# Routing of an expert-choice layer: a root moved to ScalarE and GpSimd, two conversions moved, fewer count products

## The chip, the cores and the metric

One core of a Trainium2 chip runs the whole layer in one launch. The metric is device time in microseconds (us). The runs of the kernel before have a median of 971.08 us.

The engines are TensorE (PE in the profile, its weight loads PEld), VectorE (DVE), ScalarE (ACT), GpSimd (POOL), and SyncE (SP), whose queue issues nearly all transfers. Each engine takes its instructions in the order in which the program gives them; a wait at the head of an engine's order holds everything behind it.

## The reference

An encoder layer on 512 tokens of 1024 features, in float32. Three attention branches are gated, summed and projected; the result is added to the residual and normalised. A mixture of 16 experts follows, in which each expert chooses its 64 best tokens, and a second normalisation. What this change touches lies between the two:

```python
x = layer_norm(DN_ALPHA * x + mix, ln1_g, ln1_b)          # mix = merged @ w_out
logits = jnp.einsum('btd,de->bte', x, w_router)
aff = jax.nn.softmax(logits, axis=-1)
gate, idx = lax.top_k(jnp.swapaxes(aff, 1, 2), 64)        # per expert
xs = x[bidx, idx]                                         # gathered tokens
h = jnp.einsum('becd,edf->becf', xs, w_gate_up)
hg, hu = jnp.split(h, 2, axis=-1)
ye = jnp.einsum('becf,efd->becd', jax.nn.silu(hg) * hu, w_down) * gate[..., None]
x = layer_norm(DN_ALPHA * x + zeros.at[bidx, idx].add(ye), ln2_g, ln2_b)
```

## The kernel before

Tokens stand in four chunks of 128 partitions. The order of work on every engine is written out by hand; no scheduler moves anything.

**Expert weights.** They come through a ring of twelve buffers, 2 MB or 1 MB each (class `Ring`, the transfers at L817). The queue of SyncE issues them in order, each when the buffer's last user is done. The first twelve are issued before the experts start; some of their buffers hold data of the routing first. The last of the twelve goes into the buffer of the normalised tokens `X1`, so it waits until the last chunk has been converted (L1073, the low parts). The next transfer goes into the ring's first buffer again and waits for the first two gate-and-up products (`gate_up`, L1285).

**Projection and statistics.** `w_rest` (L1104) does the second half of the output projection, chunk by chunk; the last chunk in two pieces of 256 columns. `wo_evac` (L1009) takes a piece out of PSUM, adds the residual and takes the statistics; `row_scale` (L1014) joins them and finds one over the root of the variance. It starts from an integer estimate and does three Newton steps: nine small operations on VectorE after the joining of the statistics. For the third chunk (`s2`) they alternate with the first rounds of the sort. `norm_cols` (L1060) makes the columns by which the tokens are normalised, on GpSimd; `x1_norm` (L1066) normalises a chunk on ScalarE.

**Router.** `r_transpose` (L989) transposes tokens on PE and copies them out by ScalarE; `r_logits` multiplies them with the router's weights; `affinity` (L1037) scales the logits on VectorE, takes the exponential on ScalarE and divides on VectorE. `r_back` (L1052) transposes the affinities of a chunk, so that experts lie on partitions, and ScalarE copies them out.

**Sort.** `rounds` (L1111) finds the 64 largest of each expert, eight at a time, on VectorE: first over chunks 0 and 1 (`seg`, beside the projection), then over chunks 2 and 3 with the first result's 64 (L1184 on). The 64th largest of each expert is `cut` (L1189). ScalarE makes a diagonal matrix `dg` of the cuts, and a product with ones spreads it over all partitions (`thp`, L1193).

**Counts.** VectorE compares affinities with the cut (L1197, L1198). PE counts chosen tokens ahead of each token by products with triangular and full matrices of ones: 16 products of 32 columns and 16 of 16 (L1202, L1205). VectorE turns the counts into positions and one-hot matrices (L1207 to L1223), and the gather is a product with these (`gather`, L1245 with the high parts of the tokens, L1247 with the low parts).

**High and low parts.** `x1_parts` (L1069) converts a normalised chunk to 16 bits on ScalarE (`XH`, L1070), and GpSimd subtracts and converts what is left (`XL`, two halves of 512, L1073).

**Keeping PE warm.** `keep_warm(n)` puts n products into PE's order whose result nobody reads. In the trace each shows as two matmuls.

Of the kernel before, what the change touches and what calls it, by code (L numbers as in the profile page):

```python
# [18 lines left out]
P = 128  # L19
# [3 lines left out]
NT = 4  # L23
NEXP = 16
# [40 lines left out]
def layer_kernel(ctx: ExitStack, tc: tile.TileContext, xt, xn, first0, wu, bgate, rpb, gains, wrt,  # L65
# [22 lines left out]
    def small(shape, name, dt=F32, bufs=2):  # L88
        return sp.tile(shape, dt, name=name, tag=name, bufs=bufs)
# [883 lines left out]
    def x1(m):  # L973
        return X1[:, m]
# [7 lines left out]
    nc.gpsimd.memset(a23, 0.0)  # L982
    top = cp.tile([48, 64], F32, name="top")

    XT, LG = {}, {}
    mvs, rs_v, rs_h, rs_y, rs_a, nmx, sme, rce = (
        small([P, NT, 2] if n == "mv" else [P, NT], "r_" + n, bufs=1) for n in ("mv", "v", "h", "y", "a", "nm", "sm", "rc"))
# [26 lines left out]
    def row_scale(ms, nq):  # L1014
        c = slice(ms[0], ms[-1] + 1)
        for m in ms:
            nc.vector.bn_aggr(mvs[:, m], st_all[:, m, :nq])
        yield
        v, hv, y, a = rs_v[:, c], rs_h[:, c], rs_y[:, c], rs_a[:, c]
        nc.vector.tensor_scalar(v, mvs[:, c, 1], LN_EPS, None, op0=ALU.add)  # L1020
        yield
        nc.vector.tensor_scalar(y.bitcast(I32), v.bitcast(I32), -0.5, RSQRT_SEED, op0=ALU.mult, op1=ALU.add)
        nc.vector.tensor_scalar(hv, v, -0.5, None, op0=ALU.mult)
        yield
        for i in range(3):
            if len(ms) == 1:
                nc.vector.tensor_scalar(a, y, hv, y, op0=ALU.mult, op1=ALU.mult)
                yield
                nc.vector.tensor_scalar(y, a, 1.5, y, op0=ALU.add, op1=ALU.mult)
            else:  # L1030
                nc.vector.tensor_tensor(a, y, y, op=ALU.mult)
                nc.vector.tensor_tensor(a, a, hv, op=ALU.mult)
                yield
                nc.vector.scalar_tensor_tensor(y, a, 1.5, y, op0=ALU.add, op1=ALU.mult)
            yield

    def affinity(ms):  # L1037
        ex = {m: LG[m][:, NEXP:2 * NEXP] for m in ms}
        for m in ms:
            nc.vector.scalar_tensor_tensor(lgA[:, m], LG.pop(m)[:, :NEXP], rs_y[:, m:m + 1], rb, op0=ALU.mult,  # L1040
                                           op1=ALU.add)
        c = slice(ms[0], ms[-1] + 1)
        nc.vector.tensor_reduce(nmx[:, c], lgA[:, c], axis=AX.X, op=ALU.max, negate=True)
        for m in ms:
            nc.scalar.activation(ex[m], lgA[:, m], AF.Exp, bias=nmx[:, m:m + 1], accum_out=sme[:, m:m + 1])
        yield
        nc.vector.reciprocal(rce[:, c], sme[:, c])
        for m in ms:
            nc.vector.scalar_tensor_tensor(aff[:, m], ex[m], rce[:, m:m + 1], ones_f[:, :NEXP], op0=ALU.mult, op1=ALU.mult)
        yield  # L1050

    def r_back(m):  # L1052
        ap = PB("Y", f"ap{m}")
        nc.tensor.transpose(ap[:NEXP, :P], aff[:, m], ident)
        p = 32 * (m % 2)
        nc.scalar.copy(a01[p:p + NEXP] if m < 2 else a23[p:p + NEXP, 64:], ap[:NEXP, :P])
# [3 lines left out]
    def norm_cols(ms):  # L1060
        c = slice(ms[0], ms[-1] + 1)
        nc.gpsimd.tensor_scalar(r13[:, c], rs_y[:, c], X_SCALE, None, op0=ALU.mult)
        for m in ms:
            nc.gpsimd.tensor_scalar(nb_t[:, m:m + 1], mvs[:, m, 0:1], r13[:, m:m + 1], -1.0, op0=ALU.mult, op1=ALU.mult)

    def x1_norm(m):  # L1066
        nc.scalar.activation(x1(m), x1(m), AF.Identity, bias=nb_t[:, m:m + 1], scale=r13[:, m:m + 1])

    def x1_parts(m):  # L1069
        nc.scalar.copy(XH[:, m], x1(m))  # L1070
        for h in range(2):
            c = slice(h * 512, h * 512 + 512)
            nc.gpsimd.tensor_tensor(XL[:, m, c], x1(m)[:, c], XH[:, m, c], op=ALU.subtract)  # L1073
# [66 lines left out]
    all_of(row_scale((0, 1), 2))  # L1140
    norm_cols((0, 1))
    w_rest(2, 0, 512, 1, {1: lambda: r_transpose(1, 4), 2: lambda: r_logits(1, 4),
                          3: lambda: all_of(affinity((0, 1)))})
    s2 = row_scale((2,), 2)
    seg = rounds(a01, 0, a23[:, 0:64], True)

    def sort_first():
        for _ in range(8):
            steps(s2, seg)

    w_rest(3, 0, 256, 1, {0: lambda: r_back(0), 1: then(lambda: r_back(1), sort_first), 2: lambda: r_transpose(2, 4),
                          3: lambda: r_logits(2, 4)})
    all_of(s2)
    x1_norm(0)
    norm_cols((2,))
    f2 = affinity((2,))

    def third():
        x1_norm(1)
        steps(f2)  # L1160
        all_of(seg)
        all_of(f2)

    w_rest(3, 256, 256, 2, {1: then(lambda: r_transpose(3, 4, 2), third), 2: lambda: r_logits(3, 4, 2)})
    keep_warm(3)
    r_transpose(3, 6, 2)
    r_back(2)
    r_logits(3, 6, 2)
    keep_warm(11)
    x1_parts(0)  # L1170
    all_of(row_scale((3,), 3))
    norm_cols((3,))
    all_of(affinity((3,)))
    r_back(3)
    x1_parts(1)
    for m in (2, 3):
        x1_norm(m)
        x1_parts(m)
    keep_warm(31)
    ring.upto(len(RING))  # L1180
    dump("aff", aff)

# [6 lines left out]
    nc.vector.tensor_reduce(cut, rev, axis=AX.X, op=ALU.min)  # L1189
    dg = cp.tile([NEXP, NEXP], F32, name="dg")  # L1190
    nc.scalar.activation(dg, ident[:NEXP, :NEXP], AF.Copy, scale=cut)
    thp = PB("S", "thp")
    nc.tensor.matmul(thp[:, :NEXP], ones_f[:NEXP], dg, start=True, stop=True)  # L1193
    keep_warm(1)
    msk = cp.tile([P, NT, 2, NEXP], F16, name="msk")
    thb = thp[:, None, :NEXP].to_broadcast([P, NT, NEXP])
    nc.vector.tensor_tensor(msk[:, :, 0], aff, thb, op=ALU.is_gt)  # L1197
    nc.vector.tensor_tensor(msk[:, :, 1], aff, thb, op=ALU.is_equal)  # L1198
    cnp = PB("S", "cnp", (P, NT, 2, NEXP))
    for m in range(NT):  # L1200
        for k in range(NT):
            nc.tensor.matmul(cnp[:, m].rearrange("p a e -> p (a e)"), tri_t[0 if k < m else 1 if k > m else 2],  # L1202
                             msk[:, k].rearrange("p a e -> p (a e)"), start=(k == 0), stop=False)
        for k in range(NT):
            nc.tensor.matmul(cnp[:, m, 1], ones_h, msk[:, k, 0], start=False, stop=(k == NT - 1))  # L1205
# [357 lines left out]
    for e in range(NEXP):  # L1563
# [71 lines left out]
    nc.vector.memset(ch[:, :, 7:9].bitcast(F32), 0.0)  # L1635
    warm_s = small([P, 1], "warm_s", bufs=1)
    nc.scalar.activation(warm_s, eps, AF.Sqrt)
    down(NEXP - 2, lambda: h_transpose(NEXP - 1, spare.rearrange("p (c n) -> p c n", c=4)))
    last_down(g2, {0: x0, 1: x1q}, spare)
# [141 lines left out]
```

## Time and profile before

| | us |
|---|---|
| median of 3 runs (971.02 to 971.66) | 971.08 |
| the profiled execution | 973.19 |
| its span, first to last instruction | 971.3 |
| PE busy (98% of the span) | 948.8 |
| VectorE busy (47%) | 454.8 |
| ScalarE busy (28%) | 276.0 |
| GpSimd busy (8%) | 79.3 |

Attention and projection take the first 506 us, the routing some 17 us, the experts and the last normalisation the rest. A row of the time-line has start, duration, engine, line, operation, result and operands, and in brackets the idle time before it with what ended it. A row of groups has the count, the busy time and the mean in ns, and the idle time before. Rows of windows are explained where they stand.

### The profile page before, as it was taken

Reading aid. Unit: us, or ns where it says so; the run is one execution under the profiler, and the core shown is the slowest. Engines: PE = TensorE matmul, PEld = TensorE weight load, DVE = VectorE, ACT = ScalarE, POOL = GpSimd, SP = SyncE. Lnnn points to the kernel's source line nnn. Section 1 sums busy time; section 2 is a strip of 40 time slices with the busy share of each in tenths; the row PEclk is TensorE's granted clock in tenths of the full one; section 3 lists DMA queues with packets and bytes.
Section 4 is the critical chain, followed back from the end, with each engine's and each line's share of the span. In section 5 each row is a group of like instructions: output and inputs, shape, how many; then the busy total and the mean of one; then the engine's idle time right before and its main releaser. Section 6 shows DMA issues by size and latency. Waiting matters only on the chain.

```text
span 971.3 us, 13273 instructions
## 1 busy us (share of the span) xinstructions
PE 948.8 (98%) x5444; PEld 619.5 (64%) x5444; DVE 454.8 (47%) x866; ACT 276.0 (28%) x544; POOL 79.3 (8%) x86
## 2 busy tenths in 40 slices
PE   9999999999999999999999999999999999998996
PEld 9899878889888888887886333433344333532344
DVE  6347668875376566237464122653322222231426
ACT  5334444544354454323223111100010001100123
POOL 0002303000032231000013000000000000000003
PEclk9999999999999999999999999999999999999998
DMA  9321111211333322575818999999999999999992
GB/s 360 111 68 65 65 66 44 66 46 64 85 112 112 100 82 83 218 285 201 366 61 340 406 431 430 431 430 430 431 431 429 430 431 430 430 429 430 429 396 89
DMA packets 38330, 251.21 MB, mean 259 GB/s; under 512 B 12911, under 2 KB 13295, under 8 KB 24830
## 3 DMA queue, kind: packets, MB, share of 16 engines
q1 hardware_dynamic: 37550, 249.74, 63.3%
q8 instruction: 43, 0.70, 0.3%
q10 hardware_dynamic: 720, 0.62, 0.2%
q14 instruction: 17, 0.14, 0.0%
HBM read 247.46 MB, written 2.10 MB: 257 GB/s over the span
## 4 chain that ended last, share of the span: by engine, by line
PE 80%; DMA 10%; DVE 6%; ACT 1%; issue 1%; POOL 1%; DVEq 0%; POOLq 0%; ACTq 0%; SPq 0%
DMA w<-in_wx 10%; PE g L1285 9%; PE u L1285 9%; PE y L1320 8%; PE gate L274 4%; PE gate L276 4%; PE gate L275 4%; PE pr L274 2%; PE gy L649 2%; PE ga L1245 2%; PE pr L275 2%; PE pr L276 2%; PE nqk L274 1%; PE nqk L275 1%; PE nqk L276 1%; PE gt L636 1%
## 5 line engine op out<-in xcount | busy, mean ns | idle before, releaser
L1285 PE MATMUL g<-w,xs 128*64 128x512 f32 x512 | 135.1, 606 | 3.6 <-DMA w<-in_wx 3.6
L1285 PE MATMUL u<-w,xs 128*64 128x512 f32 x512 | 131.6, 592 | 0.0
L1320 PE MATMUL y<-w,hT 128*64 128x512 f32 x480 | 106.8, 594 | 4.4 <-DMA w<-in_wx 3.7
L93 DVE TENSOR_TENSOR y<-y,y 64x512 fp32r<-64x512 f32 x30 | 20.7, 689 | 134.8 <-ACT y L92 134.8
L1285 PEld LDWEIGHTS u<-w,xs 128*64 128x64 f32 x512 | 36.8, 137 | 73.1 <-issue 72.3
L92 ACT CAST y<-y 64x512 fp32r<-64x512 f32 x30 | 17.4, 579 | 226.1 <-PE y L1320 214.8
L1320 PEld LDWEIGHTS y<-w,hT 128*64 128x64 f32 x480 | 33.7, 137 | 73.8 <-issue 63.2
L93 DVE TENSOR_TENSOR los<-raw_twin,whi 128x1024 fp32r<-128x1024 f32 x43 | 54.1, 1258 | 52.5 <-ACT whi L92 52.3
L276 PE MATMUL gate<-xh,los 128*128 128x512 f32 x192 | 74.8, 390 | 0.0
L1285 PEld LDWEIGHTS g<-w,xs 128*64 128x64 f32 x512 | 30.6, 136 | 55.0 <-issue 43.3
L274 PE MATMUL gate<-xh,whi 128*128 128x512 f32 x160 | 63.5, 397 | 0.0
L275 PE MATMUL gate<-xl,whi 128*128 128x512 f32 x160 | 62.3, 390 | 0.0
L1392 DVE TENSOR_TENSOR acc<-acc,cb 128x512 f32<-128x512 f32 x56 | 35.6, 684 | 37.7 <-PE cb L1390 37.7
L92 ACT CAST whi<-raw_twin 128x1024 fp32r<-128x1024 f32 x43 | 45.1, 1049 | 8.3 <-PE wo L1085 4.4
L93 DVE TENSOR_TENSOR los<-raw_twin,los 128x1024 fp32r<-128x1024 f32 x21 | 26.5, 1260 | 35.5 <-ACT los L92 35.4
L1461 POOL TENSOR_TENSOR acc<-acc,ln2g 128x512 f32<-128x512 f32 x6 | 7.6, 1276 | 432.7 <-DVE l2s L1489 430.7
L276 PEld LDWEIGHTS gate<-xh,los 128*128 128x128 f32 x192 | 36.0, 188 | 7.7
L625 ACT ACTIVATE att_twin<-gs,nm 128x512 f32<-128x512 f32 x32 | 21.7, 683 | 52.4 <-DVE nm L624 52.4
L1295 ACT ACTIVATE tg<-g 128x512 f32<-128x512 f32 x16 | 9.5, 597 | 90.2 <-PE g L1285 90.2
L274 PEld LDWEIGHTS gate<-xh,whi 128*128 128x128 f32 x160 | 30.0, 188 | 7.1 <-issue 1.2
L275 PEld LDWEIGHTS gate<-xl,whi 128*128 128x128 f32 x160 | 30.1, 188 | 5.9
L1308 DVE COPY hT<-ht 128x512 f32<-128x512 f32 x15 | 10.4, 691 | 44.4 <-PE ht L1303 44.4
(420 smaller groups left out, 1902.4 us busy)
## 6 DMA issues: line engine op xcount, KB each, us to landing
w<-in_wx SPq DMA_DIRECT2D x89, 2048.0 KB
raw_twin<-in_wu SPq DMA_DIRECT2D x65, 512.0 KB
w<-in_wx SPq DMA_DIRECT2D x14, 1024.0 KB
raw<-in_wu SPq DMA_DIRECT2D x8, 512.0 KB
xr<-in_xt SPq DMA_DIRECT2D x4, 512.0 KB
macc<-in_xn SPq DMA_DIRECT2D x2, 1024.0 KB
first<-in_first SPq DMA_DIRECT2D x4, 384.0 KB
bf<-in_rpb SPq DMA_DIRECT2D x64, 24.0 KB
```

Of the source, the lines that this page charges most:

```text
L92: nc.scalar.copy(hi, src)
L93: nc.vector.tensor_tensor(lo, src, hi.bitcast(F32), op=ALU.subtract)
L274: nc.tensor.matmul(acc, w_h, rh[:, k], start=(k == 0), stop=False)
L275: nc.tensor.matmul(acc, w_h, rl[:, k], start=False, stop=False)
L276: nc.tensor.matmul(acc, w_l, rh[:, k], start=False, stop=(k == nk - 1))
L625: nc.scalar.activation(self.p[:, h], self.s[h], AF.Exp, bias=nm[:, h:h + 1], accum_out=self.sm[:, h:h + 1])
L649: nc.tensor.matmul(self.y[h * 64:h * 64 + 64, :P], ST["vg"][:, kc, kvh * 64:kvh * 64 + 64], self.pt[:, h, kc], start=(kc == 0), stop=(kc = ...
L1245: nc.tensor.matmul(g, XH[:, m, c], oh[:, m, sl], start=(m == 0), stop=False)
L1285: nc.tensor.matmul(GU[e][b][hf * 64:hf * 64 + 64], xs, w[b][:, hf * 512:hf * 512 + 512], start=(k == 0), stop=(k == KD - 1))
L1308: nc.vector.tensor_copy(t, tp)
L1320: nc.tensor.matmul(y[o * 64:o * 64 + 64], hT[:, c, hf * 64:hf * 64 + 64], w[j][:, o * 512:(o + 1) * 512], start=(k == 0 and j == 0), stop= ...
L1392: nc.vector.tensor_tensor(a, a, cb, op=ALU.add)
```

## The change

- The third chunk's root, all nine operations, runs on GpSimd in place of VectorE, ahead of `norm_cols` in GpSimd's order. The affinities of that chunk wait for it.
- The last chunk's root is a square root on ScalarE, a reciprocal and one Newton step on VectorE. The square root needs another activation table than the exponential, so a table is loaded before it (with a warming call, right after the third chunk's normalisation) and the exponential's again after it.
- Normalisation of chunks 1 and 2 stands earlier in ScalarE's order.
- `r_back(2)` moves behind the last logits and stands next to `r_back(3)`; on ScalarE its copy comes behind the last exponential.
- The conversions `XH` of chunks 0 and 1 run on GpSimd.
- No diagonal: the cut itself, repeated along the columns without a copy, is the stationary operand, and the identity the moving one.
- The counts are formed by 14 products of 32 to 96 columns: one stationary matrix serves several chunks, the mask being repeated.
- Fewer warming products: 2, 5 and 28 in place of 3, 11 and 31.

```diff
+    eps = small([P, 1], "eps", bufs=1)
+    nc.gpsimd.memset(eps, LN_EPS)
+    warm_s = small([P, 1], "warm_s", bufs=1)
...
         v, hv, y, a = rs_v[:, c], rs_h[:, c], rs_y[:, c], rs_a[:, c]
-        nc.vector.tensor_scalar(v, mvs[:, c, 1], LN_EPS, None, op0=ALU.add)
-        nc.vector.tensor_scalar(y.bitcast(I32), v.bitcast(I32), -0.5, RSQRT_SEED, op0=ALU.mult, op1=ALU.add)
-        nc.vector.tensor_scalar(hv, v, -0.5, None, op0=ALU.mult)
+        eng = nc.gpsimd if len(ms) == 1 else nc.vector
+        eng.tensor_scalar(v, mvs[:, c, 1], LN_EPS, None, op0=ALU.add)
+        eng.tensor_scalar(y.bitcast(I32), v.bitcast(I32), -0.5, RSQRT_SEED, op0=ALU.mult, op1=ALU.add)
+        eng.tensor_scalar(hv, v, -0.5, None, op0=ALU.mult)
         for i in range(3):
             if len(ms) == 1:
-                nc.vector.tensor_scalar(a, y, hv, y, op0=ALU.mult, op1=ALU.mult)
-                nc.vector.tensor_scalar(y, a, 1.5, y, op0=ALU.add, op1=ALU.mult)
+                eng.tensor_scalar(a, y, hv, y, op0=ALU.mult, op1=ALU.mult)
+                eng.tensor_scalar(y, a, 1.5, y, op0=ALU.add, op1=ALU.mult)
...
+    def last_scale(m, nq):
+        c = slice(m, m + 1)
+        y, a, hv = rs_y[:, c], rs_a[:, c], rs_h[:, c]
+        nc.vector.bn_aggr(mvs[:, m], st_all[:, m, :nq])
+        nc.scalar.activation(rs_v[:, c], mvs[:, m, 1:2], AF.Sqrt, bias=eps)
+        nc.vector.tensor_scalar(hv, mvs[:, m, 1:2], LN_EPS, -0.5, op0=ALU.add, op1=ALU.mult)
+        nc.vector.reciprocal(y, rs_v[:, c])
+        nc.vector.tensor_scalar(a, y, hv, y, op0=ALU.mult, op1=ALU.mult)
+        nc.vector.tensor_scalar(y, a, 1.5, y, op0=ALU.add, op1=ALU.mult)
...
-    def x1_parts(m):
-        nc.scalar.copy(XH[:, m], x1(m))
+    def x1_parts(m, copy=nc.scalar.copy):
+        copy(XH[:, m], x1(m))
...
-    s2 = row_scale((2,), 2)
+    row_scale((2,), 2)
+    norm_cols((2,))
...
         for _ in range(8):
-            steps(s2, seg)
+            steps(seg)
...
-    all_of(s2)
     x1_norm(0)
-    norm_cols((2,))
+    x1_norm(1)
     f2 = affinity((2,))
 
     def third():
-        x1_norm(1)
         steps(f2)
...
-    keep_warm(3)
+    x1_norm(2)
+    nc.scalar.activation(warm_s, eps, AF.Sqrt)
+    keep_warm(2)
     r_transpose(3, 6, 2)
-    r_back(2)
+    last_scale(3, 3)
     r_logits(3, 6, 2)
-    keep_warm(11)
-    x1_parts(0)
-    all_of(row_scale((3,), 3))
+    keep_warm(5)
+    x1_parts(0, nc.gpsimd.tensor_copy)
     norm_cols((3,))
     all_of(affinity((3,)))
+    r_back(2)
     r_back(3)
-    x1_parts(1)
-    for m in (2, 3):
-        x1_norm(m)
-        x1_parts(m)
-    keep_warm(31)
+    x1_parts(1, nc.gpsimd.tensor_copy)
+    x1_parts(2)
+    x1_norm(3)
+    x1_parts(3)
+    keep_warm(28)
...
-    cut = small([NEXP, 1], "cut", bufs=1)
+    cut = cp.tile([NEXP, NEXP], F32, name="cut")[:, :1]
     nc.vector.tensor_reduce(cut, rev, axis=AX.X, op=ALU.min)
-    dg = cp.tile([NEXP, NEXP], F32, name="dg")
-    nc.scalar.activation(dg, ident[:NEXP, :NEXP], AF.Copy, scale=cut)
     thp = PB("S", "thp")
-    nc.tensor.matmul(thp[:, :NEXP], ones_f[:NEXP], dg, start=True, stop=True)
+    nc.tensor.matmul(thp[:, :NEXP], cut.to_broadcast([NEXP, P]), ident[:NEXP, :NEXP], start=True, stop=True)
...
-    for m in range(NT):
-        for k in range(NT):
-            nc.tensor.matmul(cnp[:, m].rearrange("p a e -> p (a e)"), tri_t[0 if k < m else 1 if k > m else 2],
-                             msk[:, k].rearrange("p a e -> p (a e)"), start=(k == 0), stop=False)
-        for k in range(NT):
-            nc.tensor.matmul(cnp[:, m, 1], ones_h, msk[:, k, 0], start=False, stop=(k == NT - 1))
+    for k in range(NT):
+        nc.tensor.matmul(cnp[:, k], tri_t[2], msk[:, k], start=(k == 0), stop=False)
+    for k in range(NT):
+        for lo, hi, t in ((0, k, 1), (k + 1, NT, 0)):
+            if lo < hi:
+                nc.tensor.matmul(cnp[:, lo:hi], tri_t[t], msk[:, k:k + 1].to_broadcast([P, hi - lo, 2, NEXP]),
+                                 start=False, stop=False)
+    for k in range(NT):
+        nc.tensor.matmul(cnp[:, :, 1], ones_h, msk[:, k, 0:1].to_broadcast([P, NT, NEXP]), start=False, stop=(k == NT - 1))
...
-    eps = small([P, 1], "eps", bufs=1)
-    nc.vector.memset(eps, LN_EPS)
...
-    warm_s = small([P, 1], "warm_s", bufs=1)
```

More of the change, by code (lines that the diff above doesn't have):

```diff
@@ L1017, in row_scale @@
             nc.vector.bn_aggr(mvs[:, m], st_all[:, m, :nq])
-        yield
         v, hv, y, a = rs_v[:, c], rs_h[:, c], rs_y[:, c], rs_a[:, c]
-        nc.vector.tensor_scalar(v, mvs[:, c, 1], LN_EPS, None, op0=ALU.add)
-        yield
-        nc.vector.tensor_scalar(y.bitcast(I32), v.bitcast(I32), -0.5, RSQRT_SEED, op0=ALU.mult, op1=ALU.add)
-        nc.vector.tensor_scalar(hv, v, -0.5, None, op0=ALU.mult)
-        yield
+        eng = nc.gpsimd if len(ms) == 1 else nc.vector
+        eng.tensor_scalar(v, mvs[:, c, 1], LN_EPS, None, op0=ALU.add)
+        eng.tensor_scalar(y.bitcast(I32), v.bitcast(I32), -0.5, RSQRT_SEED, op0=ALU.mult, op1=ALU.add)
+        eng.tensor_scalar(hv, v, -0.5, None, op0=ALU.mult)
         for i in range(3):
             if len(ms) == 1:
-                nc.vector.tensor_scalar(a, y, hv, y, op0=ALU.mult, op1=ALU.mult)
-                yield
-                nc.vector.tensor_scalar(y, a, 1.5, y, op0=ALU.add, op1=ALU.mult)
-            else:
[L1031 to L1035, printed above, removed]
+                eng.tensor_scalar(a, y, hv, y, op0=ALU.mult, op1=ALU.mult)
+                eng.tensor_scalar(y, a, 1.5, y, op0=ALU.add, op1=ALU.mult)
+            else:
+                eng.tensor_tensor(a, y, y, op=ALU.mult)
+                eng.tensor_tensor(a, a, hv, op=ALU.mult)
+                eng.scalar_tensor_tensor(y, a, 1.5, y, op0=ALU.add, op1=ALU.mult)
+    def last_scale(m, nq):
[7 more added lines that the diff above has]
+        nc.vector.tensor_scalar(y, a, 1.5, y, op0=ALU.add, op1=ALU.mult)
     def affinity(ms):
@@ L1139, in layer_kernel @@
     w_rest(1, 0, 512, 1, {1: lambda: r_transpose(0, 4), 3: lambda: r_logits(0, 4)})
-    all_of(row_scale((0, 1), 2))
+    row_scale((0, 1), 2)
     norm_cols((0, 1))
```

## The prediction

> **What bounds the kernel now.** I read the windows first, then the time-line around the routing, then the waits of the queue that loads the expert weights. Windows: start and end, PE, PEld, DVE, ACT and POOL busy, PEclk, DMA share, GB/s.
>
> ```profile
> span 971.3 us, 13273 instructions
> ...
> 518.90:520.00 1.10, 1.08 (x34) 0.90 (x34) 0.27 (x2) 0.00 (x0) 0.50 (x1) 1.00 0.10 30
> ...
> 526.00:528.00 2.00, 2.00 (x16) 0.79 (x14) 0.00 (x0) 0.37 (x1) 0.00 (x0) 1.00 0.04 16
> ...
> 530.00:541.00 11.00, 11.00 (x69) 4.02 (x70) 2.12 (x9) 2.01 (x5) 0.00 (x0) 1.00 0.99 380
> 528.00:943.00 415.00, 406.38 (x2044) 155.47 (x2042) 125.77 (x223) 47.20 (x86) 0.00 (x0) 1.00 1.01 428
> ```
>
> From 528 to 943 the DMA engines are full at 428 GB/s. PE also counts as busy nearly throughout, but it cannot finish before the last weights land, so the end is the moment at which the stream restarts, plus the rest of the weights, plus a tail that this change barely touches. Before 528 there are two holes: 518.9 to 520.0 and 526 to 528.
>
> ```profile
> 521.79 0.38 PE L1247 MATMUL ga<-oh,xhl 128*128 128x128 f16 x4
> 522.01 0.39 PE L1245 MATMUL ga<-oh,xhl 128*128 128x128 f16 x4
> ...
> 522.68 1.08 PE L1285 MATMUL g<-w,xs 128*64 128x512 f32 x4
> ...
> 526.01 1.03 PE L1285 MATMUL u<-w,xs 128*64 128x512 f32 x4
> ```
> ```profile
> SPq L817 <- POOL xhl L1073: 2.4, 1, 2.4
> ```
>
> The second hole ends when the first 2 MB ring block has been used: its last matmul ends at 526.01 + 1.03 = 527.04, and data flow again at 528. The first hole ends when GpSimd has written the last of the low parts (the queue waits 2.4 us for it; that load is the last one into the ring). So an earlier first gate matmul (522.68) moves the restart and the end one for one, as long as the load held by GpSimd has landed before the restart. That load fills the 6 us from 520 to 526. If it started right at 518.9 it would land before 525, so up to about 3 us of gain the DMA engines set no limit. What sets 522.68 is a chain through the routing. I cost each edit on this chain.
>
> **Third chunk's root off VectorE.** Times are start and duration.
>
> ```profile
> 498.84 0.21 DVE L1017 BATCH_NORM_AGGREGATE r_mv<-rt 128x2 f32<-128x12 f32 x1
> ...
> 502.88 0.20 DVE L1029 TENSOR_SCALAR r_y<-r_a,r_y 128x1 f32<-128x1 f32 x1
> 503.11 0.23 DVE L1040 SCALAR_TENSOR_TENSOR rt<-lg,r_y,rt 128x16 f32<-128x16 f32 x1
> ...
> 506.09 0.41 DVE L1011 SCALAR_TENSOR_TENSOR macc<-macc,woc 128x256 f32<-128x256 f32 x1
> ```
> ```profile
> 505.53 0.28 PE L1085 MATMUL woc<-wlast,ml 128*128 128x256 f32 x1
> ```
> ```profile
> 503.17 0.22 POOL L1062 TENSOR_SCALAR lnr<-r_y 128x1 f32<-128x1 f32 x1 [8.10 <-DVE r_y L1029]
> 503.48 0.27 POOL L1064 TENSOR_SCALAR lnnb<-r_mv,lnr 128x1 f32<-128x1 f32 x1
> ```
>
> The last projection matmul ends at 505.53 + 0.28 = 505.81, but VectorE takes its result only at 506.09, being behind with sort rounds and the root. Eight of the nine root operations stand where VectorE catches up by 502.08 anyway; the ninth, at 502.88, costs its pitch of 0.23 (502.88 to 503.11). Without it the evacuation starts at 505.86: **gain 0.23**, at most 0.28.
>
> The new wait: the logits' scaling (503.11, then 502.88) waits for nine one-column operations on GpSimd, and behind it in VectorE's order stand four sort rounds and the evacuation of the last chunk. Dependent one-column operations on GpSimd are 0.31 apart (503.17 to 503.48). Two pointer operands may make some 0.42, so nine take 2.8 to 3.3: from 499.14 to 501.9 or 502.4. The cover is 0.5 to 1.0; beyond it each microsecond on GpSimd is one at the end.
>
> **Last chunk's root.** Nine VectorE operations become a square root on ScalarE, a reciprocal and two operations of a Newton step (the fifth VectorE operation hides beside the square root).
>
> ```profile
> 507.00 0.24 DVE L1017 BATCH_NORM_AGGREGATE r_mv<-rt 128x2 f32<-128x18 f32 x1
> 507.09 0.37 ACT L996 COPY x1T<-x1t 128x256 f32<-128x256 f32 x1 [2.20 <-PE x1t L994]
> ...
> 507.36 0.25 ACT L1056 COPY a<-ap 16x128 f32<-16x128 f32 x1
> ...
> 508.83 0.27 DVE L1027 TENSOR_SCALAR r_a<-r_y,r_h 128x1 f32<-128x1 f32 x1
> 509.13 0.21 DVE L1029 TENSOR_SCALAR r_y<-r_a,r_y 128x1 f32<-128x1 f32 x1
> 509.45 0.23 DVE L1040 SCALAR_TENSOR_TENSOR rt<-lg,r_y,rt 128x16 f32<-128x16 f32 x1
> ...
> 509.93 0.28 ACT L1045 ACTIVATE lg<-rt,r_nm 128x16 f32<-128x16 f32 x1 [1.37 <-DVE r_nm L1043]
> ```
> ```profile
> 931.72 1.28 ACT L1637 ACT_TABLE_LOAD   x1
> 933.34 0.20 ACT L1637 ACTIVATE warm_s<-eps 128x1 f32<-128x1 f32 x1 [0.34 <-DVE ch L1635]
> ...
> 959.66 0.30 ACT L1513 ACTIVATE l2v<-l2mv,eps 128x4 f32<-128x4 f32 x1 [1.88 <-DVE l2mv L1511]
> ```
> ```profile
> 960.02 0.17 DVE L1517 RECIPROCAL l2y<-l2v 128x4 f32<-128x4 f32 x1
> 960.23 0.16 DVE L1518 TENSOR_TENSOR l2a<-l2y 128x4 f32<-128x4 f32 x1
> ```
>
> Everything is 0.23 earlier, so the statistics are ready at 507.01 and ScalarE starts the transposed copy at 506.86. It takes its next operation 0.27 after (507.09 to 507.36): square root at 507.13. Its nearest row is the one-column square root of 0.20 at 933.34; the hand-over to VectorE is 0.06 (959.66 + 0.30 to 960.02). So the reciprocal starts at 507.39, the Newton step at + 0.21 (960.02 to 960.23), its second half at + 0.30 (508.83 to 509.13), the scaling of the logits at + 0.32 (509.13 to 509.45): 508.22, against 509.45. The exponential follows 0.48 later: 508.70. The table load for the exponential starts when the square root ends, 507.33, and takes 1.28: 508.61, hidden by 0.09. If the 0.34 between the load and the next operation at 933.34 belonged to the load, the exponential would start at 508.95. **Gain at the exponential, with the 0.23: 509.93 - 508.70 = 1.23**; ends 0.98 and 1.32 (the load alone).
>
> The other table load, before the square root, must fit between the third chunk's normalisation and the transposed copy.
>
> ```profile
> 503.36 1.25 ACT L1067 ACTIVATE macc<-macc,lnnb,lnr 128x1024 f32<-128x1024 f32 x1
> ```
>
> In the new order the third chunk's exponential takes the slot at 503.4 in which the second normalisation stood (with its sum about 0.4, an estimate from the 0.28 at 509.93), and the third normalisation (1.25) runs from 503.8 to 505.05; load to 506.33; warming square root, 0.20, to 506.53; the copy is due at 506.86. It fits with 0.33 to spare.
>
> [...]
>
> The transposition of the third chunk's affinities moves behind the last logits, and its copy behind the last exponential: some 509.1 to 509.4, before the last chunk's transposition (about 509.7). Free. The sort has the same rounds.
>
> **No diagonal.**
>
> ```profile
> 517.78 0.21 DVE L1189 TENSOR_REDUCE cut<-rev 16x1 f32<-16x64 f32 x1
> ```
> ```profile
> 518.03 0.31 ACT L1191 ACTIVATE dg<-ident,cut 16x16 f32<-16x16 f32 x1 [0.53 <-DVE cut L1189]
> ```
> ```profile
> 518.39 0.29 PEld L1193 LDWEIGHTS thp<-dg,rt 16*128 16x128 f32 x2 [0.45 <-ACT dg L1191]
> ```
> ```profile
> 506.56 0.20 PEld L994 LDWEIGHTS x1t<-ident,macc 128*128 128x128 f32 x2 [0.27 <-DVE macc L1011]
> ```
>
> The cut ends at 517.99; ScalarE and two hand-overs lie before 518.39. Straight from VectorE to PE takes 0.06 (506.09 + 0.41 to 506.56), up to 0.12: 518.05 to 518.11. **Gain 0.31**, 0.28 to 0.34.
>
> **14 count products for 32.**
>
> ```profile
> 519.22 0.18 PE L1202 MATMUL cnp<-msk,tri_d 128*128 128x32 f16 x1
> ...
> 519.92 0.24 PE L1205 MATMUL cnp<-msk,ones_h 128*128 128x16 f16 x4
> ```
>
> Thirty-two products start from 519.22 to about 519.99, 0.025 apart whatever their 32 or 16 columns. A wide one goes by columns: four of 128 columns take 0.22 (521.79 to 522.01), 0.43 ns each. The new first thirteen are four of 32 columns (0.025 each), six of 96, 32, 64, 64, 32 and 96 (0.041, 0.025, 0.028, twice over, 0.19 in all) and three of 64 (0.08): 0.37 in place of 0.77. **Gain 0.40**, 0.30 to 0.45.
>
> **Two conversions to GpSimd.** They leave ScalarE, where they weren't late; the question is whether GpSimd becomes late.
>
> ```profile
> L1073 POOL TENSOR_TENSOR xhl<-macc,xhl 128x512 f16<-128x512 f32 x8 | 9.0, 1155 | 6.0 <-ACT xhl L1070 6.0
> ...
> L268 POOL TENSOR_SCALAR gT<-lnT 128x8 f32<-128x8 f32 x1 | 1.1, 1120 | 0.2 <-DMA lnT<-in_lnt 0.2
> ...
> L245 POOL TENSOR_SCALAR consts<-consts 128x64 f32<-128x64 f32 x1 | 0.4, 400 | 24.0 <-DMA consts<-in_gains 24.0
> masks.py:199 POOL TENSOR_SCALAR_AFFINE_SELECT ident<-ident 128x128 f32<-128x128 f32 x1 | 0.3, 292 | 0.1
> ```
>
> No row has this conversion (128x1024). From below: 128 elements in 0.29 against 0.22 for one column, about 0.6 ns each, 0.8 us. From above: 64 elements took 0.40, so 0.18 more than one column, 2.9 ns each, 3.1 us. I take 1.3: the two-input rows (1155 ns for 512, so 2.3 us for 1024 with two reads) are nearest in size, and this has one read for two. [...]
>
> GpSimd now starts when the last projection matmul frees the buffer, 505.9, 2.7 earlier than before. Its queue: conversion, two subtractions, two small operations, conversion, six subtractions: 505.9 + 2 x 1.3 + 8 x 1.155 - 0.1 + 0.6 = 518.2. The gather needs the last low part at 521.79 - 1.9 = 519.9, so the cover is 1.7 us; it is gone at 2.15 per conversion, and at 3.1 GpSimd ends at 521.8. With 1.3 the held load follows at 518.9 without a hole.
>
> **Sum.** 1.23 + 0.31 + 0.40 = 1.94 us earlier at the first gate matmul, 520.74, and at the restart (526.1). Nothing downstream takes it back: PE and DMA both start from there. The profiled execution took 973.19 against its span of 971.3; the runs' median is 971.08. I subtract from the median: 971.08 - 1.94 = 969.1; a profiled span of 969.4. The ends of the terms sum to 1.56 and 2.11, with the runs' spread: 968.7 to 969.8. For the chances, 0.2% is 1.94 us, about what a measurement of this kernel can tell from no change; the forecast sits on that bound.
>
> **Rivals.**
> *Table changes cost more than their row.* If each took twice its 1.28, the first would end at 505.05 + 2.57 + 0.20 = 507.8, the copy would be 0.96 late, the square root end at 508.3 and the exponential start at 510.9: 0.9 later than before, less the 0.71 of the other edits: 971.3. For it: two changes stand on a tight path. Against: 931.72. [...] Chance 0.06.
>
> *Conversions late.* Between 2.15 and 3.1 us each, GpSimd delivers after 519.9 and each 0.1 costs 0.2 at the gather: 969.3 to 971.1. For it: the 2.9 ns slope. Against: the affine select. Chance 0.06.
>
> *More than the sum.* From 530 to 541 the stream ran at 380 against 428 GB/s, 11 x 48 / 428 = 1.2 us lost. If that is the late held load's doing, landing it before 525 regains it: 967.9. Against: those loads are issued one by one, as PE frees blocks. Chance 0.14.
>
> *Slower: the third chunk's root stalls VectorE.* If GpSimd's operations take what its first small one took (1.12), nine last 10.1 us, to 509.2, and the scaling due at 502.88 holds sort and evacuation: 6.3 later, less 1.94: 975.5. It decides from 0.42 each on (nine in the 3.74 from 499.14 to 502.88), cancels the gain at 0.63 and passes 0.2% slower at 0.85. For: one operation works on integers, of which no GpSimd row exists. Against: 0.22 and 0.27. Chance 0.10.
>
> **Numbers.** Forecast 0.64, of which 0.34 beyond 0.2% and 0.30 short of it. Faster 0.34 + 0.14 = 0.48; within 0.2%: 0.30 + 0.06 + 0.06 = 0.42; slower 0.10. Range 968.0 to 971.3: it leaves out the slower rival and the edge of the better one.
>
> **What would show it.** Right: evacuation at 505.86, exponential at 508.7, no gap after its table load, weight load of the cut within 0.12 of its reduction, counts read 0.6 after the first product, GpSimd done by 518.9, the hole at 518.9 closed and data flowing again at 526.1. Wrong: VectorE idle at 502.9 waiting for GpSimd; the transposed copy later than 506.9; the gather waiting for the low parts; or the restart early and the end not.

## The result: 967.9 us, a quarter of a per cent faster

| kernel | median, us | runs | lowest and highest |
|---|---|---|---|
| before | 969.77 | 9 | 968.86 to 971.66 |
| after | 967.90 | 9 | 967.16 to 969.25 |

The ratio is 0.9975, with a 95% interval of 0.9966 to 0.9983: 2.4 us (1.6 to 3.3) of 969.77. The medians differ by 1.87. The forecast gain was 1.94; the forecast time was 969.1 with a range from 968.0, so the time fell 0.1 below the range. The three runs of the kernel before known at the prediction had a median of 971.08; with nine it is 969.77.

The profiled execution of the kernel after took 967.9 us, with a span of 966.1. Its windows, with the columns as in the prediction:

```profile
518.90:520.00 1.10, 1.10 (x8) 0.29 (x4) 0.47 (x3) 0.16 (x1) 0.00 (x0) 1.00 1.00 402
...
522.40:523.90 1.50, 1.50 (x14) 0.65 (x12) 0.00 (x0) 0.33 (x1) 0.00 (x0) 1.00 0.19 76
530.00:541.00 11.00, 11.00 (x70) 4.03 (x68) 3.55 (x11) 1.56 (x4) 0.00 (x0) 1.00 0.96 375
```

The first hole is closed: the DMA share from 518.9 to 520 is 1.00, where it was 0.10, and the lowest microsecond from 512 to 521 is 0.72, against 0.11 in the kernel before. The second stands earlier and ends at about 523.9, 5.3 after the first gate matmul at 518.62; before it ended at 528, 5.3 after 522.68. From 530 to 541 the stream is as slow as it was (375 against 380 GB/s). Counted from the first gate matmul the same eleven microseconds are those from 526 to 537, and there it ran at 383.

The time-line of the same kernel around the routing, TensorE first (last matmul of the projection, spread of the cut, first count products, first gate matmul), then VectorE:

```profile
503.36 0.28 PE L1093 MATMUL woc<-wlast,ml 128*128 128x256 f32 x1
...
514.71 0.39 PE L1200 MATMUL thp<-ident,cut 16*128 16x16 f32 x2 [0.59 <-DVE cut L1198]
...
515.54 0.25 PE L1208 MATMUL cnp<-msk,tri_d 128*128 128x32 f16 x4
...
518.62 1.08 PE L1295 MATMUL g<-w,xs 128*64 128x512 f32 x4
```
```profile
500.70 0.22 DVE L1048 SCALAR_TENSOR_TENSOR rt<-lg,r_y,rt 128x16 f32<-128x16 f32 x1
...
503.67 0.42 DVE L1014 SCALAR_TENSOR_TENSOR macc<-macc,woc 128x256 f32<-128x256 f32 x1
...
506.37 0.17 DVE L1051 TENSOR_REDUCE r_nm<-rt 128x1 f32<-128x16 f32 x1
...
514.44 0.21 DVE L1198 TENSOR_REDUCE cut<-rev 16x1 f32<-16x64 f32 x1
...
515.13 0.22 DVE L1204 TENSOR_TENSOR msk<-rt,thp 128x64 f16<-128x64 f32 x1 [0.48 <-PE thp L1200]
...
516.14 0.29 DVE L1217 TENSOR_TENSOR rt<-cnp,msk 128x128 f32<-128x128 f32 x1 [0.66 <-PE cnp L1215]
```

ScalarE, from the third chunk's normalisation to the last exponential, and GpSimd, from the third chunk's root to the last low part:

```profile
501.48 1.23 ACT L1075 ACTIVATE macc<-macc,lnnb,lnr 128x1024 f32<-128x1024 f32 x1
502.73 1.28 ACT L1173 ACT_TABLE_LOAD   x1
504.02 0.20 ACT L1173 ACTIVATE warm_s<-eps 128x1 f32<-128x1 f32 x1
504.68 0.37 ACT L999 COPY x1T<-x1t 128x256 f32<-128x256 f32 x1 [0.45 <-PE x1t L997]
504.95 0.30 ACT L1039 ACTIVATE r_v<-r_mv,eps 128x1 f32<-128x1 f32 x1
505.26 1.28 ACT L1053 ACT_TABLE_LOAD   x1
506.58 0.28 ACT L1053 ACTIVATE lg<-rt,r_nm 128x16 f32<-128x16 f32 x1
```
```profile
496.96 0.23 POOL L1023 TENSOR_SCALAR r_v<-r_mv 128x1 f32<-128x1 f32 x1 [4.07 <-DVE r_mv L1020]
...
499.94 0.27 POOL L1029 TENSOR_SCALAR r_y<-r_a,r_y 128x1 f32<-128x1 f32 x1
...
503.65 1.04 POOL L1078 CAST xhl<-macc 128x1024 f16<-128x1024 f32 x1 [2.79 <-ACT macc L1075]
...
508.78 6.74 POOL L1081 TENSOR_TENSOR xhl<-macc,xhl 128x512 f16<-128x512 f32 x6
```

The mask and the reading of the counts in the kernel before:

```profile
518.81 0.22 DVE L1197 TENSOR_TENSOR msk<-rt,thp 128x64 f16<-128x64 f32 x1 [0.82 <-PE thp L1193]
...
520.20 0.29 DVE L1207 TENSOR_TENSOR rt<-cnp,msk 128x128 f32<-128x128 f32 x1 [1.03 <-PE cnp L1205]
```

The projection ended at 503.64 here and at 505.81 in the profile of before, so the two are compared from that moment. Each row of this table is a difference of two starts or ends above and in the prediction:

| us | before | after | gain | forecast |
|---|---|---|---|---|
| end of projection to its evacuation | 0.28 | 0.03 | 0.25 | 0.23 |
| end of projection to last exponential | 4.12 | 2.94 | 1.18 | 1.23 |
| reduction of the cut to the mask | 1.03 | 0.69 | 0.34 | 0.31 |
| first count product to the counts read | 0.98 | 0.60 | 0.38 | 0.40 |
| counts read to first gate matmul | 2.48 | 2.48 | 0 | 0 |
| end of projection to first gate matmul | 16.87 | 14.98 | 1.89 | 1.94 |

(The evacuation is part of the second line.) The third chunk's root, the diagonal and the count products were not undone singly; for their gains of 0.25, 0.34 and 0.38 these rows stand alone.

### The profile page after: what moved, and what is told of

The parts are those of the page before. It is cut to its first block, busy times and chain, and to the rows that moved or that the text cites. A ratio compares the mean times of both kernels' runs of the same rounds, so it can differ in the third digit from the quotient of the medians.

```text
span 966.1 us, 13195 instructions
## 1 busy us (share of the span) xinstructions
PE 943.5 (98%) x5406; PEld 615.1 (64%) x5406; DVE 453.0 (47%) x851; ACT 277.2 (29%) x545; POOL 84.6 (9%) x98
## 4 chain that ended last, share of the span: by engine, by line
PE 80%; DMA 10%; DVE 6%; ACT 1%; issue 1%; POOL 1%; DVEq 0%; POOLq 0%; ACTq 0%; SPq 0%
DMA w<-in_wx 10%; PE g L1295 10%; PE u L1295 9%; PE y L1330 8%; PE gate L274 4%; PE gate L275 4%; PE gate L276 4%; PE pr L274 2%; PE gy L649 2%; PE ga L1255 2%; PE pr L275 2%; PE pr L276 2%; PE nqk L274 2%; PE nqk L276 2%; PE nqk L275 2%; PE gt L636 1%
```

## The experiments

The yardstick is the last line of that table, called the stretch, read in each kernel's one profile. What follows the first gate matmul up to the end of the span is 447.0 to 449.0 in all fourteen profiles, without a pattern by edit: 448.6 and 447.5 in two profiles of the kernel before, 447.5 and 448.0 in two of the kernel after.

| kernel | stretch, us | projection ends | span | time, us (ratio to before, 95%) |
|---|---|---|---|---|
| before | 16.87 | 505.81 | 971.3 | 969.77 |
| before_again | 16.87 | 504.21 | 968.6 | 970.48 (1.0003, 0.9995 to 1.0012) |
| after | 14.98 | 503.64 | 966.1 | 967.90 (0.9975, 0.9966 to 0.9983) |
| after_again | 14.99 | 503.40 | 966.4 | 967.67 (0.9977, 0.9968 to 0.9985) |
| u_root | 15.93 | 503.43 | 966.4 | 968.89 (0.9990, 0.9982 to 0.9999) |
| u_conv | 15.90 | 503.32 | 966.4 | 968.20, one run |
| root_back (the same program as u_root) | 15.92 | 503.46 | 967.2 | 968.98, one run |
| nowarm | 17.36 | 503.40 | 968.7 | 970.47, one run |
| no_newton | 14.97 | 503.37 | 966.0 | 967.78, one run |
| third_slow | 19.11 | 503.57 | 970.4 | 972.19, one run |
| conv_slow | 17.86 | 503.68 | 970.5 | 972.35, one run |
| delay | 18.98 | 504.37 | 971.2 | 972.83 (1.0032, 1.0021 to 1.0043) |
| delay_warm | 18.04 | 503.96 | 970.5 | 971.25 (1.0011, 1.0002 to 1.0020) |
| rev_dve | 15.01 | 503.66 | 966.1 | 968.65 (0.9983, 0.9975 to 0.9992) |

### Both kernels once more (before_again, after_again)

Neither is edited.

> The kernel before, unchanged, for a second profile. The first profile of it lay at 971.3 us of span, and against the kernel after it lost 2.17 us ahead of the last projection matmul, where the two programs do the same work, and 1.15 us between the first gate matmul and the last weights. Theory: these 3.3 us belong to the execution and not to the program (a dip of the granted clock near 120 us; the rate of the weight stream). Then this profile has the last projection matmul's end nearer 503.6 than 505.8, the stretch from there to the first gate matmul again at 16.87 (within 0.05), and a span of 968 to 971. Rival: the program before itself is slower there; then 505.8 and 419.4 come back. Ratio to the kernel before: 1.000.

> The kernel after, unchanged, timed beside the kernel before on one chip. Theory: 1.9 us faster, all of it between the end of the last projection matmul and the first gate matmul (14.98 again, against 16.87): ratio 0.9980 with an interval that holds it. Rival: more than the sum, 2.4 us or 0.9975, part of it outside that stretch; then the stretch from the first gate matmul to the last weights is shorter than in the kernel before of the same chip by 0.5 us or more.

Both came as expected: the stretch repeats to 0.01 us in both kernels, and the ratio of 0.9977 has 0.9980 in its interval. The time before the stretch does not repeat. In the first profile of before the projection ended 1.6 later than in the second. The matmul at which the loss begins, in the first profile, and the windows that hold the loss, of the first profile and then of the second:

```profile
122.88 1.01 PE L406 MATMUL rT<-ident,ropevg 128*128 128x128 f32 x4 [1.84 <-POOL ropevg L400]
```
```profile
120.00:125.00 5.00, 3.16 (x13) 2.37 (x12) 1.92 (x2) 0.58 (x1) 2.83 (x2) 0.80 0.30 105
125.00:130.00 5.00, 5.00 (x21) 4.06 (x20) 2.89 (x5) 1.47 (x4) 0.00 (x0) 0.86 0.00 0
```
```profile
120.00:125.00 5.00, 3.21 (x17) 2.42 (x16) 2.10 (x2) 0.71 (x3) 2.80 (x2) 1.00 0.29 105
125.00:130.00 5.00, 5.00 (x24) 4.14 (x23) 3.52 (x7) 2.92 (x7) 0.00 (x0) 1.00 0.01 3
```

The granted clock was 0.80 and 0.86 in the one and 1.00 in the other, on the same kernel, 375 us ahead of anything that the change touches: 5 x 0.20 + 5 x 0.14 = 1.7 us of TensorE time at most, an estimate from these clocks. TensorE stands idle for 1.79 to 1.84 us between 120 and 130 in six profiles (both of before, both of after, delay, u_root); only in this one the clock was then 0.50, from 123.0 to 126.4, and in the five others it was 1.00 over these ten microseconds. So the difference of the two spans (971.3 and 966.1) must not be read as gain as a whole.

### The last chunk's root and the two conversions, undone singly

u_root puts the last chunk's root back on VectorE and leaves the conversions on GpSimd:

```diff
-        eng = nc.gpsimd if len(ms) == 1 else nc.vector
+        eng = nc.gpsimd if ms == (2,) else nc.vector
...
-    nc.scalar.activation(warm_s, eps, AF.Sqrt)
...
-    last_scale(3, 3)
+    row_scale((3,), 3)
```

> The kernel after with the last chunk's root back on VectorE (nine operations, three Newton steps) and so without the two extra table loads. Theory: the exponential of the last chunk comes 3.87 us after the last projection matmul in place of 2.94, so 0.93 later, and the stretch to the first gate matmul is 15.9. Rival (the table loads eat what the shorter root brings): 15.0 to 15.2. Ratio to the kernel before 0.999, which the timing alone can hardly tell from 0.998.

u_conv undoes only the conversions:

```diff
-    x1_parts(0, nc.gpsimd.tensor_copy)
+    x1_parts(0)
...
-    x1_parts(1, nc.gpsimd.tensor_copy)
+    x1_parts(1)
```

> The kernel after with both conversions back on ScalarE, in the same places of the program. What the prediction says (they were not late there, so nothing is gained by their move): stretch 15.0. Theory now: chunk 0's conversion stands between the square root and the second table load in ScalarE's order, so load and exponential come about 1.0 us later: stretch 15.9 to 16.0, and GpSimd done earlier than in the kernel after, relative to the last projection matmul, by up to 2 us.

> The changed kernel with the last chunk's root back on VectorE (nine operations, three Newton steps), no square root on ScalarE and no table loads in the routing; the two conversions stay on GpSimd. It fills the fourth corner of a square: root moved and conversions moved 14.98 us from the last projection matmul to the first gate matmul, conversions alone undone 15.90, both undone 15.93. Theory (the two parts only pay together, since the conversions' place ahead of the exponential is idle time of ScalarE as long as the root is slow): 15.9, as with both undone, exponential 3.6 to 3.7 after the last projection matmul's end. Rival (each part has a gain of its own, the conversions 0.9 of it): 15.0. In between, each is worth its share.

The last of these expectations takes u_root for a kernel with both parts undone. It is not: root_back is the same program as u_root, to the letter, with the conversions on GpSimd, and its 15.92 repeats the 15.93 and tests nothing new. No run has both undone. The nearest thing to it is the kernel before: its 16.87, less the gains of the three other parts (0.25, 0.34 and 0.38), is 15.90.

So undoing the root costs 0.95 and undoing the conversions 0.92, as expected for u_root and u_conv, and undoing both, worked out in this way, costs no more than either. Each part pays only beside the other; that neither pays alone rests on the kernel before and not on a run of its own. ScalarE in u_conv shows why the fast root does not pay without the conversions' move; GpSimd and ScalarE in root_back, then ScalarE in the kernel before, why the move does not pay without the fast root:

```profile
504.83 1.03 ACT L1078 CAST xhl<-macc 128x1024 f16<-128x1024 f32 x1
505.88 1.28 ACT L1053 ACT_TABLE_LOAD   x1
507.18 0.28 ACT L1053 ACTIVATE lg<-rt,r_nm 128x16 f32<-128x16 f32 x1
```
```profile
503.48 1.04 POOL L1078 CAST xhl<-macc 128x1024 f16<-128x1024 f32 x1 [2.79 <-ACT macc L1075]
```
```profile
507.34 0.28 ACT L1053 ACTIVATE lg<-rt,r_nm 128x16 f32<-128x16 f32 x1 [2.46 <-DVE r_nm L1051]
```
```profile
507.51 1.04 ACT L1070 CAST xhl<-macc 128x1024 f16<-128x1024 f32 x1
```

In u_conv the conversion stands between the square root and the second table load, so the load ends at 507.16, 3.84 after the projection, instead of 2.90. In root_back ScalarE is idle for 2.46 us while VectorE works through nine root operations: a conversion of 1.04 would have fitted there. In the kernel before one stands there, and ScalarE is still idle for 1.37 before its exponential. Both exponentials come 3.86 to 3.88 after the projection's end, as in before without its late evacuation (4.12 - 0.25). One part of the expectation for u_conv failed: GpSimd was not done earlier but later, 13.3 after the projection's end against 11.9.

### No warming of the square root's table (nowarm)

```diff
     x1_norm(2)
-    nc.scalar.activation(warm_s, eps, AF.Sqrt)
     keep_warm(2)
```

> The kernel after without the warming square root, so the first table load stands directly ahead of the real square root, on the path. Theory (a table change costs its 1.28 us row and nothing else): the square root ends 1.4 us later than in the kernel after, the second load follows it, and the last chunk's exponential comes 2.94 + 1.4 = 4.3 us after the last projection matmul; stretch to the first gate matmul 16.4. [...] Second rival (the warming call is idle insurance): 15.0.

ScalarE, TensorE and a window of this kernel:

```profile
504.83 1.28 ACT L1039 ACT_TABLE_LOAD   x1
...
506.44 1.28 ACT L1053 ACT_TABLE_LOAD   x1
507.75 0.28 ACT L1053 ACTIVATE lg<-rt,r_nm 128x16 f32<-128x16 f32 x1
```
```profile
508.76 0.27 PE L1062 MATMUL ap<-ident,rt 128*16 128x128 f32 x1 [1.96 <-DVE rt L1057]
508.87 8.04 PE L1144 MATMUL warm<-ident 128*128 128x128 f32 x56
516.84 0.39 PE L1199 MATMUL thp<-ident,cut 16*128 16x16 f32 x2
```
```profile
510.00:511.00 1.00, 1.00 (x7) 1.00 (x7) 0.90 (x5) 1.00 (x2) 1.00 (x2) 0.50 0.99 418
```

The price of one table change is as expected: the exponential starts 507.75 - 503.40 = 4.35 after the projection, 1.41 later than in the kernel after: a load of 1.28, which starts 0.02 after the copy ahead of it, and the square root 0.01 after the load. The stretch grew by 2.38, though, to 17.36 where 16.4 was expected. TensorE was idle for 1.96 us, and from about 509.6 to 513 the granted clock was 0.50. The 56 warming matmuls, 6.42 us in the kernel after, took 8.04, and the spread of the cut, whose cut was there at 515.82, stands behind them in TensorE's order until 516.84: 1.0 us more.

### The Newton step (no_newton)

This kernel leaves out the one Newton step of the last chunk's root.

```diff
         nc.vector.reciprocal(y, rs_v[:, c])
-        nc.vector.tensor_scalar(a, y, hv, y, op0=ALU.mult, op1=ALU.mult)
-        nc.vector.tensor_scalar(y, a, 1.5, y, op0=ALU.add, op1=ALU.mult)
```

> The kernel after with the Newton step of the last chunk's root left out (the root is the reciprocal of ScalarE's square root alone). Theory: the scaling of the logits comes 0.5 to 0.6 us earlier, but the exponential still waits for its table load (which ended at 506.54 in the kernel after, the exponential starting at 506.58), so the stretch stays at 14.98, within 0.05. Rival (VectorE's chain alone sets the exponential): 14.4 to 14.5.

```profile
505.76 0.17 DVE L1049 TENSOR_REDUCE r_nm<-rt 128x1 f32<-128x16 f32 x1
```
```profile
505.00 1.28 ACT L1051 ACT_TABLE_LOAD   x1
506.29 0.28 ACT L1051 ACTIVATE lg<-rt,r_nm 128x16 f32<-128x16 f32 x1
```

VectorE has the maximum ready at 505.93, and the exponential still starts at 506.29, when the load is over. In the kernel after, load and maximum both end at 506.54. So the Newton step is free here, and a faster root would gain nothing: the load sets the exponential, as expected.

### The third chunk's root made longer (third_slow)

Six Newton steps on GpSimd for the third chunk in place of three:

```diff
-        for i in range(3):
+        for i in range(6 if len(ms) == 1 else 3):
```

> The kernel after with six Newton steps in place of three in the third chunk's root on GpSimd: six operations more, about 2.43 us (0.44 + 0.37 a step). Theory (the prediction's slower rival, with the cover that the trace of the kernel after shows, 0.45 us): VectorE stands idle before the scaling of the third chunk's logits, sort and last evacuation come 2.0 us later, stretch 17.0. Rival (the sort has room, or the wait is hidden): 15.0 to 15.5.

VectorE and TensorE:

```profile
502.62 0.23 DVE L1048 SCALAR_TENSOR_TENSOR rt<-lg,r_y,rt 128x16 f32<-128x16 f32 x1 [1.90 <-POOL r_y L1029]
```
```profile
506.06 0.44 PE L997 MATMUL x1t<-ident,macc 128*128 128x128 f32 x2 [2.05 <-DVE macc L1014]
...
507.59 2.48 PE L1144 MATMUL warm<-ident 128*128 128x128 f32 x10
...
510.80 8.04 PE L1144 MATMUL warm<-ident 128*128 128x128 f32 x56
518.77 0.39 PE L1200 MATMUL thp<-ident,cut 16*128 16x16 f32 x2
```

VectorE waits 1.90 for GpSimd, as the prediction's slower rival has it: beyond the cover a microsecond on GpSimd is one at the evacuation. The stretch grew by 4.13 instead of 2.0, and the rest comes with the clock again: 2.05 us without work for TensorE, then a granted clock of 0.50 from about 507.5 to 514. Ten warming matmuls took 2.48 instead of 1.36 and held the transposition of the affinities, so that the sort began 1.2 later still; the cut then waited 0.9 longer behind the other 56.

### GpSimd made late (conv_slow)

```diff
+    for _ in range(4):
+        nc.gpsimd.tensor_copy(XH[:, 0], x1(0))
     x1_parts(0, nc.gpsimd.tensor_copy)
```

> The kernel after with chunk 0 converted four times more on GpSimd ahead of the real conversion (same result), 4 x 1.12 = 4.5 us more on GpSimd. Theory: GpSimd's last low part is done 16.4 us after the last projection matmul (11.9 in the kernel after), 2.2 later than the gather needs it, so the stretch grows from 14.98 to about 17.2; the cover is 2.3 us. Rival (the low parts have no cover, each microsecond on GpSimd costs one): 19.5. Rival (the low parts are never waited for): 15.0.

VectorE, GpSimd and TensorE:

```profile
514.78 0.22 DVE L1198 SCALAR_TENSOR_TENSOR rev<-rev,top 16x64 f32<-16x64 f32 x1 [0.83 <-ACT rev L1197]
...
517.07 0.73 DVE L1221 TENSOR_TENSOR msk<-rt 128x64 f32<-128x64 f32 x1
517.84 2.70 DVE L1235 TENSOR_TENSOR oh<-iota_t,msk 128x128 f16<-128x128 f32 x4
```
```profile
513.23 6.76 POOL L1081 TENSOR_TENSOR xhl<-macc,xhl 128x512 f16<-128x512 f32 x6
```
```profile
519.04 0.22 PE L1257 MATMUL ga<-oh,xhl 128*128 128x128 f16 x1 [1.35 <-DVE oh L1235]
```

It came later than expected (17.86, not 17.2), and not by the expected way: the gather waits for the one-hot matrices, not for the low parts. First ScalarE, whose last normalisation waits 2.94 for a column of GpSimd, copies the sorted values late (VectorE waits 0.83 for it, 0.27 in the kernel after). Then, while GpSimd subtracts until 519.99, VectorE's position operation takes 0.73 and the four one-hots 2.70; in the kernel after, with GpSimd done at 515.52, they take 0.22 and 0.90. The operation just ahead of them, which reads one of its two operands from PSUM, takes 0.29 in both. Both operands of the slow ones are in SBUF; why these slow down and that one does not, no run shows. So the cover of GpSimd's queue ends when those operations start, at 516.47 in the kernel after, some 0.95 us after GpSimd is done there.

### What a late cut costs, and what an idle TensorE costs (delay, delay_warm)

The join of the two sorted lists, repeated on the same result, in TensorE's idle time and then with 26 more warming matmuls in it:

```diff
-    nc.vector.scalar_tensor_tensor(rev, rev, 1.0, top[:NEXP], op0=ALU.mult, op1=ALU.max)
+    for _ in range(13):
+        nc.vector.scalar_tensor_tensor(rev, rev, 1.0, top[:NEXP], op0=ALU.mult, op1=ALU.max)
```
```diff
-    keep_warm(28)
+    keep_warm(41)
```

> The kernel after with the step that joins the two halves of the sorted lists repeated 12 more times on VectorE (each depends on the one before, same result). Theory (the end follows the first gate matmul one for one): 12 x 0.25 = 3.0 us more between last projection matmul and first gate matmul (18.0), the stretch from the first gate matmul to the last instruction unchanged at 447.5 to 448.6, time 3.0 us over the kernel after, 1.1 over the kernel before (ratio 1.0011). Rival (the weight stream sets the end by itself): the first gate matmul 3.0 later, the stretch behind it shorter by 1 us or more, and a time less than 2 us over the kernel after.

> As the delayed kernel (12 more joining steps on VectorE, 3.0 us), with 41 warming products in place of 28 before it, so PE does not stand idle for 3.6 us. Without them the stretch was 18.98, 1.0 more than the 12 steps account for, and the granted clock fell to 0.5 in the gather. Theory (idle time on PE costs the clock, and the clock that 1.0 us): no fall of the clock, stretch 18.0, time 3.0 over the kernel after (ratio to the kernel before about 1.001, against 1.0032). Rival (the 1.0 us is the delay's own): 19.0 again.

TensorE and a window of delay, then the same window of delay_warm:

```profile
518.49 0.39 PE L1201 MATMUL thp<-ident,cut 16*128 16x16 f32 x2 [3.64 <-DVE cut L1199]
```
```profile
520.00:521.00 1.00, 1.00 (x8) 1.00 (x6) 0.77 (x4) 0.00 (x0) 0.00 (x0) 0.50 1.05 426
```
```profile
520.00:521.00 1.00, 1.00 (x8) 0.57 (x7) 0.97 (x5) 0.00 (x0) 0.00 (x0) 1.00 0.97 393
```

Delay came out at 18.98 where 18.0 was expected. With the idle 3.64 us filled (0.74 of it is left), the clock stays at 1.00 and the stretch is 18.04: the added 3.06 us on VectorE shift the end one for one, and the idle time costs another 0.94. In the timed runs it is 1.0032 against 1.0011, each measured against before on a chip of its own. That is 2.0 us, more than the 0.94 of the two profiles. Five of delay's seven runs had a mean granted clock of 0.993, its profiled one 0.996, and none of delay_warm's less than 0.995; where in the kernel those runs lost the rest, no trace shows.

### The reversal of the sorted list on VectorE (rev_dve)

```diff
-    nc.scalar.copy(rev, top[32:48, ::-1])
+    nc.vector.tensor_copy(rev, top[32:48, ::-1])
```

> The kernel after with the copy of the reversed list (ahead of the join) on VectorE in place of ScalarE, a candidate for a better version. Theory: two hand-overs between engines go (0.04 and 0.02 us) and the copy itself takes 0.14 to 0.2 of pitch in place of 0.23: stretch 14.85 to 14.95, nothing that the timing can tell from the kernel after (ratio to the kernel before 0.9976). Rival: VectorE's read across partitions is slower, stretch 15.0 or more.

The stretch is 15.01, as the rival has it: no gain. The copy takes 0.25 to the next operation on VectorE (0.23 on ScalarE). No kernel tried has a stretch shorter than the one after by more than the 0.01 to which it repeats.

## Why the prediction was right, and where it was wrong

**The sum was right.** All of its terms came within 0.05 us, the total 1.89 against 1.94, and the gain by timed runs (2.4, interval 1.6 to 3.3) holds it. The remaining 0.5 between 1.89 and 2.4 lies inside the interval and is not located: what follows the first gate matmul is not shorter in the profiles of the kernel after (447.5, 448.0) than in the second of before (447.5).

**The step that failed is the base.** "I subtract from the median: 971.08 - 1.94 = 969.1", with "the runs' spread" put on the ends of the range: three runs within 0.64 us were taken for the spread of the kernel, and the base was 1.31 too high. Nine runs reach from 968.86 to 971.66; thirty more, on another chip, have a median of 969.93. From 969.77 the same sum gives 967.8, and 967.9 was measured. The profiled span went wrong in the same way: 969.4 was forecast from the one profile known, 966.1 came, and from the second profile's 968.6 the sum gives 966.7. A sign was in the profile: the windows from 120 to 130 us had a granted clock of 0.80 and 0.86, where before_again, both profiles of after, delay and u_root have 1.00. Whether the three timed runs lost time in the same place, no trace shows.

**The moved root.** The forecast times hold when shifted by the 2.17 us by which the projection ended earlier: transposed copy due at 506.86, seen at 504.68; exponential at 508.70, seen at 506.58. Only small sizes were off: the square root took 0.30 at one column (0.20 taken) and the exponential, with load and maximum both ready at 506.54, started 0.04 later. The first table load has 0.46 to spare (0.33 forecast). The rival "table changes cost more than their row" is out: both loads take 1.28, they start 0.02 and 0.01 after the operation ahead, and the next operation 0.01 and 0.04 after them. The load at 931.72 in the kernel before, the rival's "Against", starts 0.01 after its tanh:

```profile
931.11 0.60 ACT L1295 ACTIVATE tg<-g 128x512 f32<-128x512 f32 x1 [5.79 <-PE g L1285]
```

**The third chunk's root.** From 496.96 to 500.21 it takes 3.25, inside the forecast 2.8 to 3.3, and VectorE uses it at 500.70 without waiting. The slower rival's mechanism exists (third_slow), but GpSimd is not that slow: the integer operation takes 0.19, the eight others 0.21 to 0.35, and those with two pointer operands stand 0.44 to 0.45 ahead of the next (0.42 taken).

**The conversions.** They take 1.04, not 1.3, and GpSimd is done 11.9 after the projection's end (12.4 forecast). Two statements failed without moving the sum. "They leave ScalarE, where they weren't late" priced the move at nothing, and so the sum put the whole gain at the exponential down to the two roots; u_conv shows that the move is worth 0.92 once the last root is fast. And the cover was put at 1.7 us against the gather; conv_slow shows that VectorE's positions and one-hots suffer first, and by the trace of the kernel after the cover is about 1.

**More than the sum.** Landing the held load early did not bring back the rate from 530 to 541 (375 GB/s), so that rival's mechanism is absent, though its time, 967.9, is the measured one. **The bound of 0.2%.** The measured gain of 0.25% lies beyond it, its interval (0.17% to 0.34%) on both sides, as the forecast put it.

## What to carry to other kernels

Compare two profiles from the last moment that the change cannot touch: here that stretch repeated to 0.01 us while the whole time moved by 2 to 3, so that the relative sum could be read from one profile each and the absolute one not from three runs. Price two parts that share an engine as a pair: undoing either the fast root or the conversions' move lost some 0.9 us, the gain of the pair. Filler work that stands in an engine's order is a bound of its own: without it the 3.64 us of idle time in delay cost 0.94, and it holds whatever stands behind it when it runs slow (the cut's spread by 1.0 us in nowarm).

## What the runs showed of the hardware

- An idle time of TensorE of 1.96, 2.05 and 3.64 us was followed by a granted clock of 0.50, for 3.4 us in nowarm and delay and 6.8 in third_slow (the 2.05), and so were two of 1.35 and 0.94 with one product between (conv_slow, whose first gate matmuls took 1.97 for 1.08); a single one of 1.49 us (u_root) left it at 1.00. The length alone does not decide: 1.84 us near 122 us was followed by 0.50 for 3.4 us in the first profile of before, and the same 1.84 between 120 and 130 left the clock at 1.00 in u_root. Filling the 3.64 us kept it at 1.00 (delay_warm); the two shorter ones were not filled for a test.
- While GpSimd subtracted two operands (conv_slow, until 519.99), VectorE operations with both operands in SBUF took about three times as long as in the kernel after (one 0.73 against 0.22, four 2.70 against 0.90), one with an operand in PSUM as long (0.29), and GpSimd's own six as long (6.76 against 6.74).
- A conversion of 128x1024 from 32 to 16 bits took GpSimd 1.04 us, as long as ScalarE (1.03 to 1.05).
- Repeating a stationary column over 128 columns without a copy cost nothing that shows: 0.39 for the spread of the cut and 0.29 for its weight load in both kernels.
